# Gate columns of the modulation as running sums on VectorE instead of column-tiled products on TensorE

## Chip, cores and metric

One core of one Trainium2 chip runs the kernel. The metric is the device time of one execution in microseconds; three runs of the kernel before gave 3354.97, 3355.01 and 3358.41 us, with a median of 3355.01 us.

## What is computed

One layer of a diffusion block over 384 token columns: 128 context tokens (prompt) and 256 latent tokens (sample). Everything is float32. Cut to what matters:

```python
mod = silu(c_ctx) @ w_ada + b_ada        # prompt;  sample: silu(c) @ w_ada + b_ada
shift, scale, gate = split(mod, 3)       # each 4096 wide; w_ada is 4096 x 12288
u = rms_norm(h, norm_w) * (1 + scale) + shift
proj = u @ w_in                          # 4096 x 16448: inputs of 8 retention and 16 delta-rule heads, and 64 gate columns
mixed, states = mixers(proj)             # two bidirectional recurrences in chunks, with a triangular solve
h = h + gate * (mixed @ w_out)           # w_out is 4096 x 4096
y = rms_norm(h, final_norm_w)
```

The change is about `gate`: 4096 columns of `mod`, for two conditioning vectors (prompt and sample). They are needed only in the last line, when the output projection's columns are finished, 512 at a time.

## The kernel before

**Weights.** Every large product is split in two parts for precision. A piece is one block of 128 rows of weights by 512 columns. SyncE (SP) loads two pieces at a time into a tile `raw` (ring of three, L197), ScalarE rounds it to `wh` (L209), VectorE forms the remainder `wl = raw - wh` (L210), and TensorE runs nine matmuls of 512 columns (kind N, L264 to L266) or twelve of 384 (kind T, L258 to L260) on a piece. `wh` and `wl` have rings of five (`RING`), and `run_pieces` (L347) writes the loads and splits of a piece into the program up to four pieces ahead of its matmuls. All engines work their instructions strictly in program order; SP runs as far ahead as ring slots come free.

**Stages.** First (to about 770 us) the shift and scale columns of `mod` and the first parts of the input projection run together; class `Ada` (L301) makes the products with `w_ada`, from a ring `adar` of six tiles of 512 KB. Then `open_mixers` starts the mixer stage: the 32 groups of columns of `w_in` are finished in eight periods p = 0 to 7 of four groups each, two of kind T and two of kind N. Since some parts were done in the first stage, the periods hold 56, 128, 96, 84, 108, 100, 96 and 112 pieces. Last comes the output projection: eight blocks of 512 columns with 32 pieces each, `w_out`.

**Background work.** The mixers of period p (generators `gdn` and `ret`) are put into the program between the matmuls. `slot(ns)` advances a planned TensorE time; whenever the planned time of a background step has passed, `bg_step` writes the next one. Each `yield ns` gives a step's expected VectorE time; `pace` multiplies it by 1.4 and by a factor from 0.5 to 1 that depends on when the result is due. A piece counts 1920 ns, and an `Ada` piece 450 ns. Background work and `wl` share VectorE, in program order. The longest VectorE part is the triangular solve, `gdn` L851 to L857: 30 steps of one TENSOR_TENSOR (L854) and one TENSOR_REDUCE (L856) each, after a wait for the tile `M` that comes back from DRAM through the GpSimd (POOL) queue. Below, "a solve" is the stretch from its first to its last VectorE instruction; there is one in each period.

**Gate columns before.** `Ada` also makes the gate columns, in the N groups of the mixer stage: eight blocks of 512 columns, 16 pieces each, 128 pieces in all. A piece loads 512 rows by 256 columns (512 KB) into a slot of the ring `raw`, and runs

```python
for q in range(4):
    k = i % NK + q
    PE.matmul(self.ps[32 * q:32 * q + 32, cs], cst[:, 2 * k:2 * k + 32], raw[:, q, 0], ...,
              tile_position=(0, 32 * q))
```

on four column tiles of the array (L322; eight matmuls in the trace, since a float32 product takes two). These pieces take one of the four places for prepared pieces, and their `raw` slot comes free only when TensorE has run them. At the end of a block, `gate_done` copies the four partial sums out (L1178), adds them up with a 0/1 matrix `sel` (L1184), fetches the bias with two DMAs on the POOL queue (L1188), adds it on VectorE (L1191) and writes `d_gate` to DRAM (L1192). These steps are "urgent": they go ahead of other background steps.

**Output.** For every block of 512 output columns, `pre` (in `out_done`) loads `d_gate` five pieces before the block's end.

Of the kernel before, what the change touches and what calls it, by code (L numbers as in the profile page):

```python
# [7 lines left out]
F32 = mybir.dt.float32  # L8
F32R = mybir.dt.float32r
AF = mybir.ActivationFunctionType  # L10
ALU = mybir.AluOpType
# [4 lines left out]
D = 4096  # L16
NK = 32
T = 384
# [23 lines left out]
ADA_RING = 6  # L42
RAW_LIVE = 8
SLOT = 1000.0
PRE = 5
RING = 5
PACE = 1.4
# [5 lines left out]
GATE = 1500  # L53
# [6 lines left out]
LEAD = 3  # L60
WAIT1 = 5000
# [4 lines left out]
def hybrid_step(ctx: ExitStack, tc: tile.TileContext, x_prompt, x_sample, state_ret_fwd, state_ret_bwd,  # L66
# [35 lines left out]
    half_c = const.tile([128, 2, 12], F32, name="half_c")  # L102
    mid_ctx = ExitStack()
# [5 lines left out]
    cst = mid.tile([128, 2 * NK + 32], F32, name="cst")  # L109
    sel = mid.tile([128, 2], F32, name="sel")  # L110
# [10 lines left out]

    G.memset(half_c[:, 0], -0.5)
# [68 lines left out]

    def load_piece(src, chunks, k0, nk, ring=None):
        shape = [128, nk, len(chunks), chunks[0][1]]
        if ring:
            raw = ring(shape)
        else:
            raw = wpool.tile(shape, F32, tag="raw", name="raw", bufs=3)  # L197
        for i, (c0, cn) in enumerate(chunks):
            SP.dma_start(out=raw[:, :, i, :],
                         in_=src[k0 * 128:(k0 + nk) * 128, c0:c0 + cn].rearrange("(k p) n -> p k n", p=128))  # L200
        return raw

    def split_tile(raw, shape, place=None):
# [5 lines left out]
        A.copy(h, raw)  # L209
        V.tensor_tensor(lo, raw, h.bitcast(F32), op=ALU.subtract)  # L210
        return h, lo
# [89 lines left out]
    class Ada:  # L301
# [6 lines left out]
        def __init__(self, c0, width, ps_alloc, done, ring=None):  # L308
# [7 lines left out]
        def compute(self, i, raw):  # L316
            if self.ps is None:
                self.ps = self.ps_alloc()
            cs = slice(256 * (i // NK), 256 * (i // NK) + 256)
            for q in range(4):  # L320
                k = i % NK + q
                PE.matmul(self.ps[32 * q:32 * q + 32, cs], cst[:, 2 * k:2 * k + 32], raw[:, q, 0],  # L322
                          start=(k < 4), stop=(k >= NK - 4), tile_position=(0, 32 * q))
# [23 lines left out]
    def run_pieces(pieces):  # L347
# [9 lines left out]
        kind = lambda o: "do" if isinstance(o, Do) else ("ada" if isinstance(o, Ada) and o.ring else "w")  # L357
# [14 lines left out]
    crow = st.tile([64, 128], F32, name="crow")  # L372
# [5 lines left out]
    V.tensor_copy(sel, con[:, C_SEL:C_SEL + 2])  # L378
# [9 lines left out]
    brow = st.tile([64, 128], F32, name="brow")  # L388
    nrow = st.tile([32, 128], F32, name="nrow")
    grow = st.tile([1, 128], F32, name="grow")  # L390
# [280 lines left out]
    def gates(graw):  # L671
# [4 lines left out]
        par = mx.tile([128, 5, 16], F32, tag="mix", name="par", bufs=2)  # L676
# [63 lines left out]
    def u3(ap):  # L740
        return ap.rearrange("p (n t) -> p n t", n=3)

    def gdn(p, rt):
# [257 lines left out]
        for i, h in enumerate(heads):  # L1001
            so = mx.tile([128, 2, 128], F32, tag="mix", name="so", bufs=2)
# [45 lines left out]
        for i, h in enumerate(heads):  # L1048
# [4 lines left out]
            t = mx.tile([128, T], F32, tag="mix", name="mix", bufs=2)  # L1053
            V.scalar_tensor_tensor(out=t, in0=ps[:, 0:T], scalar=gnw[:, 0:1], in1=zT[:, i], op0=ALU.mult, op1=ALU.mult)
            G.dma_start(out=d_mix[16 + h], in_=t)
            yield

    def ret(h, rt):
# [104 lines left out]
        for a in range(2):  # L1163
# [4 lines left out]
            t = mx.tile([128, T], F32, tag="mix", name="mix", bufs=2)  # L1168
# [4 lines left out]

    def gate_done(i):
        def done(ps):
            sb = [mx.tile([128, T], F32, tag="gsb", name="gsb", bufs=2)[:, 0:256] for _ in range(2)]
            for j in range(2):
                A.copy(sb[j], ps[:, 256 * j:256 * j + 256])  # L1178
            urgent.append(fin(ps, sb))

        def fin(ps, sb):
            yield GATE
            for j in range(2):
                PE.matmul(ps[0:2, 256 * j:256 * j + 256], sel, sb[j], start=True, stop=True)  # L1184
            yield
            c0 = 512 * i
            for j in range(2):
                G.dma_start(out=sb[j][0:2], in_=b_ada[0, 2 * D + c0 + 256 * j:2 * D + c0 + 256 * j + 256].partition_broadcast(2))  # L1188
            yield 2000
            for j in range(2):  # L1190
                V.tensor_tensor(sb[j][0:2], ps[0:2, 256 * j:256 * j + 256], sb[j][0:2], op=ALU.add)  # L1191
                G.dma_start(out=d_gate[:, c0 + 256 * j:c0 + 256 * j + 256], in_=sb[j][0:2])  # L1192
        return done
# [20 lines left out]
    ada_q = []  # L1214
    for i in range(8):
        ada_q += Ada(2 * D + 512 * i, 512, lambda: ps_main.tile([128, 512], F32, tag="mm3", name="adg"), gate_done(i)).pieces
    for g, (kind, chunks) in enumerate(groups):
        k0 = reached.get(g, 0)
        pre, done = sum_done(g, ("dram" if g >= 4 else "sbuf") if k0 else None, True)
        gm = Gemm(kind, w_in, chunks, list(range(k0, NK)), done, pre)  # L1220
        if g % 4 == 0 and g:
            dues[id(gm), max(0, len(gm.pieces) - PRE)] = ("gdn", g // 4 - 1)
        if kind == "T":
            pieces += gm.pieces
        else:
            n, rest = len(gm.pieces), 0
            if g % 2:
                rest = min(8, n // 2)
                cnt = len(ada_q) - 16 * (7 - g // 4)
            else:  # L1230
                cnt = min(16, max(0, 16 * n // (n + NK - reached.get(g + 1, 0) - 8)))
            pieces += gm.pieces[:LEAD] + interleave(gm.pieces[LEAD:n - rest], ada_q[:cnt]) + gm.pieces[n - rest:]
            ada_q = ada_q[cnt:]
    assert not ada_q
# [16 lines left out]

    oc = {}
# [28 lines left out]
    def out_done(c0):  # L1281
# [3 lines left out]
        def pre():  # L1285
# [3 lines left out]
            op = oc["sb"]  # L1289
            box["x"] = op.tile([128, 3, 512], F32, tag="xo", name="xo", bufs=1)  # L1290
# [29 lines left out]

    for i in range(8):
# [7 lines left out]
        if i == 0:  # L1329
# [4 lines left out]
            for j, piece in enumerate(seq):  # L1334
# [3 lines left out]
                pieces.append(piece)  # L1338
        else:
            pieces += gm.pieces  # L1340
# [53 lines left out]
```

## Time and profile before

| what | value |
|---|---|
| median of three runs | 3355.01 us |
| profiled execution: its own time | 3351.84 us |
| profiled execution: span from first to last instruction | 3350.1 us |
| mean granted TensorE clock | 0.991 |
| mean DMA rate over the span | 187 GB/s |

The profile names an instruction group by line, engine, operation and tiles (`out<-in`). PE is the matmul row of TensorE and PEld its weight loads, DVE is VectorE, ACT ScalarE, POOL GpSimd, SP SyncE. Busy times are the union of instruction times in microseconds, means are in nanoseconds. A waits row reads "who waits <- for whom: us in total, times, longest".

### The profile page before, as it was taken

Reading aid. Unit: us, or ns where it says so; the run is one execution under the profiler, and the core shown is the slowest. Engines: PE = TensorE matmul, PEld = TensorE weight load, DVE = VectorE, ACT = ScalarE, POOL = GpSimd, SP = SyncE. Lnnn points to the kernel's source line nnn. Section 1 sums busy time; section 2 is a strip of 40 time slices with the busy share of each in tenths; the row PEclk is TensorE's granted clock in tenths of the full one; section 3 lists DMA queues with packets and bytes.
Section 4 is the critical chain, followed back from the end, with each engine's and each line's share of the span. In section 5 each row is a group of like instructions: output and inputs, shape, how many; then the busy total and the mean of one; then the engine's idle time right before and its main releaser. Section 6 shows DMA issues by size and latency. Waiting matters only on the chain.

```text
span 3350.1 us, 51853 instructions
## 1 busy us (share of the span) xinstructions
PE 3254.2 (97%) x19312; PEld 2694.5 (80%) x19312; DVE 1845.3 (55%) x3811; ACT 1201.5 (36%) x2588; POOL 292.7 (9%) x463
## 2 busy tenths in 40 slices
PE   5999999999999999999999999999999999999998
PEld 2878888877799789689689689779779877788886
DVE  3664444337747646755756746746744855444444
ACT  3322222224244344244244244245244334333333
POOL 0000000001011011001011011011000002100000
PEclk7999999999999999999999999999999999999999
DMA  9989998965535545545644545554544555645445
GB/s 327 308 289 303 324 303 282 303 189 171 160 92 151 166 138 167 167 142 150 186 145 143 172 138 152 173 156 141 172 152 142 159 153 186 188 145 169 146 150 176
DMA packets 594237, 626.14 MB, mean 187 GB/s; under 512 B 38978, under 2 KB 577042, under 8 KB 593984
## 3 DMA queue, kind: packets, MB, share of 16 engines
q1 hardware_dynamic: 570096, 551.04, 52.0%
q0 software_dynamic: 23888, 71.79, 7.2%
q8 instruction: 151, 2.47, 0.3%
q14 instruction: 102, 0.84, 0.1%
HBM read 590.37 MB, written 32.33 MB: 186 GB/s over the span
## 4 chain that ended last, share of the span: by engine, by line
PE 81%; DVE 7%; DMA 6%; issue 3%; ACT 1%; SPq 1%; POOL 0%; ACTq 0%; POOLq 0%; DVEq 0%
PE mm L258 11%; PE mm L260 10%; PE mm L259 10%; PE mm L264 10%; PE mm L265 9%; PE mm L266 9%; PE ada L322 3%; DMA raw<-in_w_in_dram 3%; DVE tmp L854 3%; PE o L265 2%; PE o L266 2%; PE o L264 2%; DVE wl L210 2%; DMA mixl<-d_mix 2%; PE adg L322 1%
## 5 line engine op out<-in xcount | busy, mean ns | idle before, releaser
L210 DVE TENSOR_TENSOR wl<-raw,wh 128x512 fp32r<-128x512 f32 x1274 | 855.3, 686 | 947.4 <-ACT wh L209 931.6
L209 ACT CAST wh<-raw 128x512 fp32r<-128x512 f32 x1274 | 757.5, 620 | 1388.5 <-DMA raw<-in_w_in_dram 567.7
L264 PE MATMUL mm<-wh,uh 128*128 128x512 f32 x1920 | 782.4, 408 | 12.3 <-ACT rawt L564 5.9
L265 PE MATMUL mm<-wl,uh 128*128 128x512 f32 x1920 | 756.5, 394 | 18.0 <-DVE wl L210 17.4
L266 PE MATMUL mm<-wh,ul 128*128 128x512 f32 x1920 | 751.6, 391 | 0.0
L258 PE MATMUL mm<-uh,wh 128*128 128x384 f32 x2048 | 716.8, 350 | 4.1 <-DVE ul L555 2.7
L260 PE MATMUL mm<-uh,wl 128*128 128x384 f32 x2048 | 685.8, 335 | 0.0
L259 PE MATMUL mm<-ul,wh 128*128 128x384 f32 x2048 | 685.1, 335 | 0.0
L264 PEld LDWEIGHTS mm<-wh,uh 128*128 128x128 f32 x1920 | 361.3, 188 | 144.9 <-issue 44.2
L265 PEld LDWEIGHTS mm<-wl,uh 128*128 128x128 f32 x1920 | 361.7, 188 | 103.5 <-DVE wl L210 36.4
L258 PEld LDWEIGHTS mm<-uh,wh 128*128 128x128 f32 x2048 | 384.7, 188 | 48.7 <-issue 25.0
L266 PEld LDWEIGHTS mm<-wh,ul 128*128 128x128 f32 x1920 | 361.1, 188 | 76.7 <-DVE ul L1249 0.3
L259 PEld LDWEIGHTS mm<-ul,wh 128*128 128x128 f32 x2048 | 385.1, 188 | 3.9 <-issue 2.9
L260 PEld LDWEIGHTS mm<-uh,wl 128*128 128x128 f32 x2048 | 384.4, 188 | 0.0
L854 DVE TENSOR_TENSOR tmp<-M 48x4 f32<-48x4 f32 (+14 forms) x240 | 188.3, 784 | 3.4
L322 PE MATMUL ada<-adar,cst 128*32 128x256 f32 x2048 | 146.8, 403 | 23.4 <-DMA adar<-in_w_ada_dram 23.4
L645 DVE SCALAR_TENSOR_TENSOR acc<-rawt,cw,acc 128x126 f32<-128x126 f32 (+3 forms) x384 | 133.5, 410 | 11.9 <-ACT acc L640 11.9
L265 PE MATMUL o<-wl,uh 128*128 128x512 f32 x354 | 138.1, 390 | 0.9 <-DVE wl L210 0.9
L264 PE MATMUL o<-wh,uh 128*128 128x512 f32 x354 | 137.9, 389 | 1.0 <-ACT wh L209 1.0
L266 PE MATMUL o<-wh,ul 128*128 128x512 f32 x354 | 137.7, 389 | 0.0
L856 DVE TENSOR_REDUCE M<-tmp 48x2 f32<-48x4 f32 (+14 forms) x240 | 121.7, 507 | 8.4
L322 PEld LDWEIGHTS ada<-adar,cst 128*32 128x32 f32 x2048 | 53.8, 112 | 88.7 <-DMA adar<-in_w_ada_dram 42.9
(321 smaller groups left out, 2522.5 us busy)
## 6 DMA issues: line engine op xcount, KB each, us to landing
raw<-in_w_in_dram SPq DMA_DIRECT2D x1028, 256.0 KB, 3.7
adar<-in_w_ada_dram SPq DMA_DIRECT2D x256, 512.0 KB, 5.4
raw<-in_w_ada_dram SPq DMA_DIRECT2D x128, 512.0 KB, 3.7
raw<-in_w_out_dram SPq DMA_DIRECT2D x256, 256.0 KB, 3.1
rawt<-d_part POOLq DMA_DIRECT2D x26, 384.0 KB, 4.3
d_part<-spill POOLq DMA_DIRECT2D x9, 768.0 KB, 6.3
gr<-d_gc POOLq DMA_DIRECT2D x16, 384.0 KB, 7.3
d_mix<-mix POOLq DMA_DIRECT2D x32, 192.0 KB, 2.8
```

Of the source, the lines that this page charges most:

```text
L209: A.copy(h, raw)
L210: V.tensor_tensor(lo, raw, h.bitcast(F32), op=ALU.subtract)
L258: PE.matmul(ps, wh, high(k), start=st, stop=False)
L259: PE.matmul(ps, wh, low(k), start=False, stop=False)
L260: PE.matmul(ps, wl, high(k), start=False, stop=sp)
L264: PE.matmul(ps, a, h, start=st, stop=False)
L265: PE.matmul(ps, a, lo, start=False, stop=False)
L266: PE.matmul(ps, b, h, start=False, stop=sp)
L322: PE.matmul(self.ps[32 * q:32 * q + 32, cs], cst[:, 2 * k:2 * k + 32], raw[:, q, 0], start=(k < 4), stop=(k >= NK - 4), tile_position=(0, ...
L645: V.scalar_tensor_tensor(out=dst[:, lo:hi], in0=x[:, lo + o:hi + o], scalar=w(t), in1=dst[:, lo:hi], op0=ALU.mult, op1=ALU.add)
L854: V.tensor_tensor(t, M[0:48, 0:i, 0:i].rearrange("p j c -> p c j"), M[0:48, i:i + 1, 0:i].to_broadcast([48, i, i]), op=ALU.mult)
L856: V.tensor_reduce(M[0:48, i, 0:i], t, axis=AX.X, op=ALU.add)
```

## The change

The class `GateSum` takes the place of `Ada` for the gate columns. A piece loads two blocks of 128 rows by 384 columns (384 KB, into `raw`). VectorE multiplies each block by the per-partition conditioning value and adds it to a running sum of 128 x 384, one for each of the two vectors: four instructions a piece, two of them (`add(0)`) written at once and two (`add(1)`) behind the next `wl`. There are eleven blocks (ten of 384 columns and one of 256) of 16 pieces, so 176 pieces and 704 instructions. When a block is full, four matmuls with a matrix of ones (each on a column tile of 32) sum over the partitions, four DMAs bring the bias, one VectorE addition and four more DMAs finish it.

One block runs in each of periods 1 to 7, spread evenly over all four groups of the period but its first 3 and last 10 pieces; the other four run in the output projection, spread over its blocks 1 to 6. `GateSum` pieces count 0 ns of planned TensorE time and no place among the prepared pieces.

To make room, the ring `raw` goes from three to four, the ring `adar` of the first stage from six to five, and several tiles of the mixers are written over others that have been read: `vn` over `vT`, `so` over `kt`, the mixed output over `zT` and over `rt["q"]`; `con2`, `par` and small start-up tiles change places. The diff, cut:

```diff
-ADA_RING = 6
+ADA_RING = 5
+RAW_RING = 4
+GATE_W = 384
+GATE_END = 10
...
-            raw = wpool.tile(shape, F32, tag="raw", name="raw", bufs=3)
+            raw = wpool.tile(shape, F32, tag="raw", name="raw", bufs=RAW_RING)
...
         A.copy(h, raw)
         V.tensor_tensor(lo, raw, h.bitcast(F32), op=ALU.subtract)
+        if later:
+            later.pop(0)()
         return h, lo
...
+    class GateSum:
+        slots = 0.0
+        def __init__(self, c0, width):
+            self.c0, self.width = c0, width
+            self.pieces = [(self, i) for i in range(0, NK, 2)]
+        def prepare(self, i):
+            raw = load_piece(w_ada, [(2 * D + self.c0, self.width)], i, 2)
+            if i == 0:
+                tag = (lambda v: f"ga{v}") if oc else (lambda v: "gsb")
+                self.acc = [(oc["sb"] if oc else mx).tile([128, T], F32, tag=tag(v), name="gacc", bufs=2)
+                            for v in range(2)]
+            def add(q):
+                for v, acc in enumerate(self.acc):
+                    a, w = acc[:, 0:self.width], cst[:, 2 * (i + q) + v:2 * (i + q) + v + 1]
+                    if i + q == 0:
+                        V.tensor_scalar(a, raw[:, q, 0], scalar1=w, scalar2=None, op0=ALU.mult)
+                    else:
+                        V.scalar_tensor_tensor(out=a, in0=raw[:, q, 0], scalar=w, in1=a, op0=ALU.mult, op1=ALU.add)
+            while later:
+                later.pop(0)()
+            add(0)
+            if i + 2 < NK:
+                later.append(lambda: add(1))
+            else:
+                add(1)
+        def compute(self, i, hl):
+            if i + 2 == NK:
+                urgent.append(self.fin())
+            return 1
+        def fin(self):
+            n, sb = self.width // 2, self.acc[0]
+            parts = [(32 * q, q // 2, n * (q % 2)) for q in range(4)]
+            yield GATE
+            ps = ps_main.tile([128, T // 2], F32, tag="mm3", name="gsum")
+            for r, v, o in parts:
+                PE.matmul(ps[r:r + 32, 0:n], ones, self.acc[v][:, o:o + n], start=True, stop=True, tile_position=(0, r))
+            yield
+            for r, v, o in parts:
+                c0 = 2 * D + self.c0 + o
+                G.dma_start(out=sb[r:r + 32, 0:n], in_=b_ada[0, c0:c0 + n].partition_broadcast(32))
+            yield 2000
+            V.tensor_tensor(sb[:, 0:n], ps[:, 0:n], sb[:, 0:n], op=ALU.add)
+            for r, v, o in parts:
+                G.dma_start(out=d_gate[v:v + 1, self.c0 + o:self.c0 + o + n], in_=sb[r:r + 1, 0:n])
+            clock["gate"] = self.c0 + self.width
...
-        kind = lambda o: "do" if isinstance(o, Do) else ("ada" if isinstance(o, Ada) and o.ring else "w")
+        kind = lambda o: "do" if isinstance(o, (Do, GateSum)) else ("ada" if isinstance(o, Ada) else "w")
...
-            t = mx.tile([128, 3, 128], F32, tag="vn", name="vn", bufs=2)
+            t = u3(vT[:, i])
...
-            so = mx.tile([128, 2, 128], F32, tag="mix", name="so", bufs=2)
+            so = kt[i][:, 0:2]
...
-            V.scalar_tensor_tensor(out=t, in0=ps[:, 0:T], scalar=gnw[:, 0:1], in1=zT[:, i], op0=ALU.mult, op1=ALU.mult)
-            G.dma_start(out=d_mix[16 + h], in_=t)
+            V.scalar_tensor_tensor(out=zT[:, i], in0=ps[:, 0:T], scalar=gnw[:, 0:1], in1=zT[:, i], op0=ALU.mult, op1=ALU.mult)
+            G.dma_start(out=d_mix[16 + h], in_=zT[:, i])
...
-            t = mx.tile([128, T], F32, tag="mix", name="mix", bufs=2)
+            t = rt["q"][:, T * a:T * a + T]
...
+    gate_sums = [GateSum(c0, min(GATE_W, D - c0)).pieces for c0 in range(0, D, GATE_W)]
+    for p in range(8):
+        gp = []
+        for g in range(4 * p, 4 * p + 4):
...
+            gp += gm.pieces
+        if p:
+            gp = gp[:LEAD] + interleave(gp[LEAD:-GATE_END], gate_sums.pop(0)) + gp[-GATE_END:]
+        pieces += gp
...
+        elif i < 7:
+            behind += gm.pieces
         else:
-            pieces += gm.pieces
+            pieces += interleave(behind, [p for ps in gate_sums for p in ps]) + gm.pieces
```

More of the change, by code (lines that the diff above doesn't have):

```diff
@@ L102, in hybrid_step @@
     half_c = const.tile([128, 2, 12], F32, name="half_c")
+    ones = const.tile([128, 32], F32, name="ones")
+    cst = const.tile([128, 2 * NK + 32], F32, name="cst")
     mid_ctx = ExitStack()
@@ L108, in hybrid_step @@
     gnw = mid.tile([128, 1], F32, name="gnw")
-    cst = mid.tile([128, 2 * NK + 32], F32, name="cst")
-    sel = mid.tile([128, 2], F32, name="sel")
     rcon = mid.tile([128, R_N], F32, name="rcon")
@@ L120, in hybrid_step @@
     rk_dec = mid.tile([128, 2, 8], F32, name="rk_dec")
+    G.memset(ones, 1.0)
     G.memset(half_c[:, 0], -0.5)
@@ L189, in slot @@
             clock["next"] = max(clock["next"], -SLOT) + bg_step()
+    oc = {}
     def load_piece(src, chunks, k0, nk, ring=None):
@@ L201, in load_piece @@
         return raw
+    later = []
     def split_tile(raw, shape, place=None):
@@ L306, in hybrid_step, with __init__ @@
         slots = 450.0
-        def __init__(self, c0, width, ps_alloc, done, ring=None):
+        def __init__(self, c0, width, ps_alloc, done, ring):
             self.c0, self.width, self.ps_alloc, self.done, self.ring = c0, width, ps_alloc, done, ring
@@ L371, in hybrid_step @@
     con = st.tile([128, C_N], F32, tag="spill", name="con", bufs=2)
-    crow = st.tile([64, 128], F32, name="crow")
+    boot = st.tile([64, 4, 128], F32, tag="spill", name="boot", bufs=2)
+    crow = boot[:, 0]
     SP.dma_start(out=con, in_=consts)
@@ L377, in hybrid_step @@
     V.tensor_copy(neg.rearrange("p d s -> p (d s)"), con[:, C_NF:C_NF + 256])
-    V.tensor_copy(sel, con[:, C_SEL:C_SEL + 2])
     def psb():
@@ L386, in hybrid_step @@
     A.activation(cst[:, 0:2 * NK].rearrange("p (k b) -> p b k", b=2), ps[:, 0:64].rearrange("p (b k) -> p b k", b=2), AF.Silu)
-    brow = st.tile([64, 128], F32, name="brow")
-    nrow = st.tile([32, 128], F32, name="nrow")
-    grow = st.tile([1, 128], F32, name="grow")
+    brow, nrow, grow = boot[:, 1], boot[0:32, 2], boot[0:1, 3]
     vrow = st.tile([120, 2, 128], F32, tag="u32", name="vrow", bufs=2)
@@ L675, in gates @@
         con = mx.tile([128, 3, 128], F32, tag="acc", name="con2", bufs=2)
-        par = mx.tile([128, 5, 16], F32, tag="mix", name="par", bufs=2)
+        par = mx.tile([128, 5, 16], F32, tag="d15", name="par", bufs=2)
         G.dma_start(out=con[:, 0:2], in_=consts[:, C_TF:C_TF + 256].rearrange("p (a b) -> p a b", a=2))
@@ L1167, in ret @@
             yield
-            t = mx.tile([128, T], F32, tag="mix", name="mix", bufs=2)
+            t = rt["q"][:, T * a:T * a + T]
             (A.copy if a else V.tensor_copy)(t, ps[:, 0:T])
@@ L1171, in ret @@
         yield
[L1174 to L1193, printed above, removed]
     def gates_done(ps):
@@ L1213, in hybrid_step @@
     pieces += Do(open_mixers).pieces + Gates(gates_done).pieces
[L1214 to L1223, printed above, removed]
-            pieces += gm.pieces
[L1225 to L1234, printed above, removed]
+    gate_sums = [GateSum(c0, min(GATE_W, D - c0)).pieces for c0 in range(0, D, GATE_W)]
+    for p in range(8):
+        gp = []
+        for g in range(4 * p, 4 * p + 4):
+            kind, chunks = groups[g]
+            k0 = reached.get(g, 0)
+            pre, done = sum_done(g, ("dram" if g >= 4 else "sbuf") if k0 else None, True)
+            gm = Gemm(kind, w_in, chunks, list(range(k0, NK)), done, pre)
+            if g % 4 == 0 and g:
+                dues[id(gm), max(0, len(gm.pieces) - PRE)] = ("gdn", g // 4 - 1)
+            gp += gm.pieces
+        if p:
+            gp = gp[:LEAD] + interleave(gp[LEAD:-GATE_END], gate_sums.pop(0)) + gp[-GATE_END:]
+        pieces += gp
     rowk = [(2 * (j // 4) if j % 4 >= 2 else 16 + 2 * (j // 4)) + j % 2 for j in range(NK)]
@@ L1249, in mix_put @@
         V.tensor_tensor(low(j), mixl[j], high(j).bitcast(F32), op=ALU.subtract)
-    oc = {}
     def open_out():
@@ L1289, in pre @@
             op = oc["sb"]
+            assert clock["gate"] >= c0 + 512
             box["x"] = op.tile([128, 3, 512], F32, tag="xo", name="xo", bufs=1)
@@ L1319, in place @@
                            for t in (uh, ul)]
+    behind = []
     for i in range(8):
```

1 line of the change is left out of this document (removed).

## Prediction

> **What bounds the kernel now.** I read the page's totals first, then one gate piece in the timeline, then the groups of instructions, a table of windows by solve and by stage, and last the waits.
>
> ```profile
> span 3350.1 us, 51853 instructions
> ...
> PE 3254.2 (97%) x19312; PEld 2694.5 (80%) x19312; DVE 1845.3 (55%) x3811; ACT 1201.5 (36%) x2588; POOL 292.7 (9%) x463
> ```
>
> TensorE's matmul row is busy nearly throughout, VectorE a little over half. So work taken off TensorE should shorten the run, as long as VectorE, in program order, still delivers `wl` in time. What a gate piece costs TensorE is read in the timeline (start, length in us, instruction).
>
> ```profile
> 776.92 0.39 PE L265 MATMUL mm<-wl,uh 128*128 128x512 f32 x1
> 777.15 0.39 PE L266 MATMUL mm<-wh,ul 128*128 128x512 f32 x1
> 777.47 0.64 PE L322 MATMUL adg<-raw,cst 128*32 128x256 f32 x8
> 778.04 0.50 PE L264 MATMUL mm<-wh,uh 128*128 128x512 f32 x1
> 778.37 0.39 PE L265 MATMUL mm<-wl,uh 128*128 128x512 f32 x1
> 778.61 0.39 PE L266 MATMUL mm<-wh,ul 128*128 128x512 f32 x1
> ```
>
> A plain step takes 0.23 (776.92 to 777.15). From the L266 before the piece to the L266 behind it, three steps on, 1.46 pass instead of 0.68. The eight matmuls and the stop and restart around them thus cost 0.78 us.
>
> ```profile
> L322 PE MATMUL adg<-raw,cst 128*32 128x256 f32 x1024 | 81.8, 391 | 2.1 <-DMA raw<-in_w_ada_dram 2.1
> ```
>
> 1024 matmuls are 128 pieces: 128 x 0.78 = 100 us of TensorE time that the change removes. That is the most that the trace prices directly.
>
> ```profile
> core 0: us, PE busy (x) PEld busy (x) DVE busy (x) ACT busy (x) POOL busy (x), PEclk, DMA share, GB/s
> ...
> sum 447.80, PE 424.59 PEld 305.33 DVE 405.04 ACT 99.87 POOL 2.04; mean PE 53.07 PEld 38.17 DVE 50.63 ACT 12.48 POOL 0.25
> ```
>
> This table has one window per solve (from its first to its last instruction on VectorE), eight in all; the sum says that VectorE is busy 405.0 of 447.8, which is 50.6 of 56.0 us in each. Here VectorE, not TensorE, is nearly full. The next three answers split those windows: the solves' own tile `M`, the gate matmuls, and `wl` in the first and the last window.
>
> ```profile
> sum 447.80, DVE 310.44 POOL 0.00; mean DVE 38.80 POOL 0.00
> ```
>
> ```profile
> sum 447.80, PE 38.40 PEld 9.41 DVE 0.82 ACT 0.64; mean PE 4.80 PEld 1.18 DVE 0.10 ACT 0.08
> ```
>
> ```profile
> 843.40:897.10 53.70, 24.73 (x61) 11.26 (x61) 14.02 (x22) 1.00 0.54 167
> ...
> 2630.80:2685.80 55.00, 27.85 (x72) 13.34 (x71) 14.13 (x22) 1.00 0.54 168
> ```
>
> Of the 50.6 us the solve takes 310.4 / 8 = 38.8, and 22 `wl` take the other 11.8, or 0.54 each. The gate matmuls' 38.4 us at 0.64 a piece are 60 pieces, 7.5 a window. TensorE's need in a window is then 22 pieces of nine steps (2.05 each, 45 us) and 7.5 x 0.78 = 5.9, together 51 of 56: it loses about 5 us in each solve already.
>
> **The change, part by part.** *Removed from TensorE:* 100 us, of which 60 x 0.78 = 47 lie in the solves and 53 outside.
>
> *Added to VectorE:* 704 instructions of 128 x 384. The trace has this operation with 126 to 255 columns on SBUF tiles and with 384 from PSUM:
>
> ```profile
> L210 DVE TENSOR_TENSOR wl<-raw,wh 128x512 fp32r<-128x512 f32 x1274 | 855.3, 686 | 947.4 <-ACT wh L209 931.6 <-PE ada L322 7.5 <-PE mm L259 2.8
> ...
> L645 DVE SCALAR_TENSOR_TENSOR acc<-rawt,cw,acc 128x255 f32<-128x255 f32 x96 | 45.8, 477 | 0.0
> ...
> L645 DVE SCALAR_TENSOR_TENSOR acc<-rawt,cw,acc 128x126 f32<-128x126 f32 x96 | 33.0, 344 | 11.9 <-ACT acc L640 11.9
> ...
> L1054 DVE SCALAR_TENSOR_TENSOR mix<-bg,gnw,rawt 128x384 f32<-128x384 f32 x16 | 9.7, 612 | 3.8 <-PE bg L1051 3.6
> ```
>
> The slope (477 - 344) / (255 - 126) = 1.03 ns a column gives 610 for 384, and L1054 shows 612. But instructions in a row overlap at their ends:
>
> ```profile
> 1010.95 2.05 DVE L645 SCALAR_TENSOR_TENSOR acc<-rawt,cw,acc 128x126 f32<-128x126 f32 x6
> 1012.92 0.69 DVE L210 TENSOR_TENSOR wl<-raw,wh 128x512 fp32r<-128x512 f32 x1
> ```
>
> Three of 0.344 and three of 0.477 are 2.46 by their lengths and 2.05 as a row, 0.07 less each. I take 0.54, so 2.16 a gate piece and 704 x 0.54 = 380 us in all, with 0.61 as the upper end. [...] The row above shows starts closer together than the lengths, so I keep to the row.
>
> Where does this go? By stage:
>
> ```profile
> 770.00:2785.00 2015.00, 1981.57 (x11682) 1656.18 (x11681) 1245.29 (x2694) 783.97 (x1791) 228.87 (x343) 1.00 0.51 154
> 2860.00:3300.00 440.00, 436.00 (x1918) 359.30 (x1917) 189.18 (x284) 146.55 (x263) 25.14 (x44) 1.00 0.52 160
> ```
>
> In the mixers VectorE is busy 1245 of 2015 us; seven blocks add 7 x 64 x 0.54 = 242 (1487). In the output projection it is 189 of 440, and four blocks add 138 (327, or 74%). On average both fit. Outside the solves the mixers go from 840 of 1567 (1245 - 405, 2015 - 448) to about 1017 of 1510. TensorE has `wl` four pieces ahead, 8 us, against crowded places such as the convolutions; I allow 10 us for new stalls there (0 to 30) and 5 in the output projection (0 to 20).
>
> *The solves are where it doesn't fit.* Periods 1 to 7 have 724 pieces, less 13 each at the ends 633, and 112 gate pieces over them: 0.18 for each piece. Background steps are placed by planned TensorE time; as 7.5 `Ada` pieces of 450 ns leave a window, 1.8 more ordinary ones enter, 23.8 in all. VectorE then needs 38.8 + 23.8 x 0.54 + 4.2 x 2.16 = 60.7 us, TensorE 23.8 x 2.05 = 48.8. VectorE is 11.9 too slow, and only the lead softens it. Part of that is gone at the start, because the solve first waits for `M`:
>
> ```profile
> ACT wh L209 <- DMA raw<-in_w_in_dram: 421.6, 125, 8.5
> ...
> PEld mm L265 <- DVE wl L210: 36.4, 54, 3.3
> ...
> DVE M L851 <- DMA M<-d_m: 31.6, 8, 6.9
> ```
>
> 31.6 / 8 = 4.0 us a solve, so 4.2 of the 8.2 us lead remain and TensorE stalls 7.7, against 5 now. In each of seven windows 5.9 is saved and 2.7 lost: 7 x 3.2 = 22. The solve of period 0 gets no gate piece; I count 8 for it, since both its gate pieces and part of its stall go.
>
> *The ring.* The first row says that ScalarE (and `wl` behind it) waits for raw weights 421.6 / 125 = 3.4 us at a time. One reason stands in SP's own waits:
>
> ```profile
> SPq L199 <- PE adg L322: 197.4, 76, 6.6
> ```
>
> Gate pieces now hold a `raw` slot until TensorE has run them, and SP can't load. After the change VectorE frees the slot, and there are four. I count 5 us for that (0 to 40, which is the 5 us of all eight solves).
>
> *The first stage* loses one of six `adar` tiles. It costs TensorE little waiting now (from 100 us to the stage's end):
>
> ```profile
>   DMA adar<-in_w_ada_dram: 7.4, 26
> ```
>
> ```profile
> adar<-in_w_ada_dram SPq DMA_DIRECT2D x256, 512.0 KB, 5.4
> raw<-in_w_ada_dram SPq DMA_DIRECT2D x128, 512.0 KB, 3.7
> ```
>
> Five tiles in flight are still nearly as many as land in 5.4 us at the stage's rate; I count 2 us lost (-5 to 10).
>
> *Finishing a block.* Four small matmuls and their stop on TensorE replace four others of the same kind:
>
> ```profile
> 882.24 1.02 PE L1184 MATMUL adg<-gsb,sel 128*2 128x256 f32 x4
> 883.20 0.50 PE L264 MATMUL mm<-wh,uh 128*128 128x512 f32 x1
> ```
>
> Eleven blocks instead of eight at some 1 us each cost 3 at most; as each product is narrower I count 0. Four bias DMAs follow each other on the POOL queue instead of two:
>
> ```profile
>   DMA gsb<-in_b_ada_dram: 5.2, 8
> ...
> L1188 POOL DMA_DIRECT2D gsb<-in_b_ada_dram x16: 499/530/574, 883.1 to 2777.8; - x16
> ...
> DMA to landing us min/median/max: 1.6/3.5/5.2
> ```
>
> 4 x 0.53 + 3.5 is 5.6 us, while the addition is written 2 us behind, so VectorE may stand still 3.6 us, with the next `wl` behind it; the lead of 8.2 covers it. I count 2 us for the eleven (40 if a block ends with no lead).
>
> *In-place tiles.* They cost no instruction. A later `rawt` now waits for the `d_mix` transfer out of it; POOL loads parts five pieces (10 us) before they are added, so a wait of the length below is covered; uncovered it would cost that much for a group, some 20 us over the periods.
>
> ```profile
> d_mix<-mix POOLq DMA_DIRECT2D x32, 192.0 KB, 2.8
> ```
>
> The loads of gate columns, 176 of 384 KB for 128 of 512, run on SP beside a half-idle DMA.
>
> Sum: 22 + 8 + 53 + 5 gained, 10 + 5 + 2 + 2 lost: 69 us. The profiled execution took 3351.8 us (1.7 outside the span), 3.2 under the median; 3355 - 69 = 3286.
>
> **Rivals.** *A: VectorE loses the lead altogether (about no change).* With 0.61 an instruction, `wl` at its full 0.69 and no lead left, a solve is 38.8 + 16.4 + 10.2 = 65.4 against 48.8: 16.6 lost, less 5 now, 81 in seven. With 20 more in the crowded places outside, 100 - 81 - 20 leaves nothing: 3355. For it speaks that the solves are 90% full now, against it that VectorE has slack on average, so the lead comes back between crowded places. [...] The timeline, with step after step at 0.23, speaks against it; I leave it 0.03 of A's chance.
>
> *B: the additions wait for their own data (slower).* `add(0)` is written right behind its load, so VectorE, in order, would wait for 384 KB to land, with all `wl` and background steps behind it. Weights make ScalarE wait 3.4 us at a time now. If each gate piece cost VectorE 3.4, a solve would lose 4.2 x 3.4 = 14 more, 100 in seven, and in the output projection 64 x 3.4 + 327 = 545 us would exceed the 440: 105 more. 3286 + 205 = 3491. It turns into a loss where the wait passes 2.3 us a piece in the solves (69 / 29.4). Against it: with four slots of two pieces, SP can start a load some 6 to 12 us before it is read, and it lands in 3.7 (above); in the output projection such waits are few today:
>
> ```profile
> ACT wh L209 <- DMA raw<-in_w_out_dram: 32.4, 14, 4.1
> ```
>
> *C: better.* If the fourth slot and the end of TensorE-held slots remove the 5 us stalls of the solves and the lead takes in the rest, the 100 us stay whole and some 10 come on top: 3245.
>
> **How the numbers follow.** My forecast 0.66, C 0.14, A 0.11, B 0.09. The range is 3238 to 3340: up to 54 us above the forecast (20 more in the crowded places, 15 more in the output projection, 8 in the first stage, some 11 where a block's end or a transfer is not covered), and 48 below (40 of the ring and 7 of the first stage), which takes C in. A and B, 0.20, stay outside. A measurement here can tell 0.2%, 7 us, from no change. Faster by more: 0.66 + 0.14 + 0.05 of A = 0.85; the same 0.05; slower 0.10 (B and the end of A).
>
> **What would show it.** The matmuls of L322 named `adg` are gone, 704 additions of about 0.6 us stand on VectorE, and VectorE's share is near 68%. In the solves VectorE is busy over 95% and TensorE waits for `wl` more than the 36.4 us of now. The waits of additions for `w_ada` transfers are short. In the output projection TensorE stays full. Wrong would be: additions that idle over 1 us each before they start (B), solves far longer than 62 us or long `wl` waits outside them (A), a first stage that ends later by over 10 us.

## The result, and the profile after

Slower. Four runs of the changed kernel have a median of 3388.94 us (3385.96 to 3392.01), four of the kernel before 3354.99 us. The ratio is 1.0099, with a 95% interval of 1.0081 to 1.0116: about 33 us lost where 69 gained were forecast, and 49 us beyond the end of the range. The profiled execution took 3386.23 us.

The page's totals after the change, and three of its rows of groups (a row ends with the engine's idle time ahead of the group and what ended it):

```profile
span 3384.5 us, 50821 instructions
...
PE 3199.1 (95%) x18344; PEld 2694.1 (80%) x18344; DVE 2179.9 (64%) x4509; ACT 1198.8 (35%) x2572; POOL 320.5 (9%) x520
...
L218 DVE TENSOR_TENSOR wl<-raw,wh 128x512 fp32r<-128x512 f32 x1274 | 854.5, 686 | 717.7 <-ACT wh L217 697.3
...
L275 PE MATMUL mm<-wl,uh 128*128 128x512 f32 x1920 | 766.4, 399 | 71.3 <-DVE wl L218 70.9
...
L362 DVE SCALAR_TENSOR_TENSOR gacc<-raw,cst,gacc 128x384 f32<-128x384 f32 (+1 forms) x682 | 379.9, 600 | 8.7 <-DMA raw<-in_w_ada_dram 8.7
```

The 968 matmuls are gone (19312 to 18344) and with them 55 us of TensorE's busy time, yet the span is 34 us longer: TensorE now stands still more. The 682 additions (the other 22 of 704 start a sum with a plain product) cost VectorE what was forecast, 380 us (379.9 in the trace), and waited only 8.7 us for their own data. So VectorE's own bill was right; what it does to TensorE was not. Of the signs that the prediction listed, these came as written: L322's matmuls gone, solves over 95% busy on VectorE and near 62 us long, short waits of additions for `w_ada`. VectorE's share is 64% where 68% was listed. Two that would be wrong came as well: a first stage that ends over 10 us later, and an output projection that is no longer full.

The answer on waits for the whole kernel (waiter, what it waited for, us in total, times, longest):

```profile
PEld mm L275 <- DVE wl L218: 114.5, 107, 3.0
...
DVE M L913 <- DMA M<-d_m: 33.9, 8, 6.2
...
DVE gacc L388 <- DMA gacc<-in_b_ada_dram: 12.7, 10, 2.0
```

TensorE's weight loads wait 114.5 us for `wl`, against 36.4 before; some 110 of the 114.5 lie in the eight solves and the 4 us behind each. The four bias DMAs of a block's end make VectorE wait 12.7 us in all.

Where the time went is read by cutting both executions at the same weight matmuls. The windows by stage (first stage, period 0, periods 1 to 7, blocks 1 to 6 of the output projection; start:end length, then busy time of each engine, granted clock, DMA share, GB/s), first of the kernel before, then of the kernel after:

```profile
0.00:769.00 769.00, 725.54 (x5223) 588.70 (x5224) 348.04 (x719) 217.18 (x434) 18.55 (x41) 0.97 0.87 288
769.00:898.50 129.50, 121.40 (x604) 85.75 (x602) 98.91 (x230) 48.47 (x115) 13.40 (x19) 1.00 0.57 173
898.50:2800.70 1902.20, 1875.06 (x11152) 1582.68 (x11153) 1155.66 (x2485) 742.00 (x1690) 218.09 (x328) 1.00 0.51 153
2876.70:3271.50 394.80, 392.91 (x1730) 324.12 (x1729) 166.10 (x248) 128.44 (x229) 17.62 (x31) 1.00 0.51 157
```

```profile
0.00:790.50 790.50, 733.82 (x5224) 594.27 (x5225) 342.33 (x719) 213.68 (x435) 18.57 (x42) 0.99 0.89 281
790.50:906.70 116.20, 105.92 (x470) 84.04 (x468) 97.42 (x228) 47.67 (x111) 11.87 (x15) 1.00 0.42 120
906.70:2810.00 1903.30, 1812.37 (x10260) 1571.10 (x10260) 1374.66 (x2921) 745.51 (x1671) 231.61 (x356) 0.99 0.49 146
2889.90:3304.50 414.60, 403.54 (x1762) 327.98 (x1761) 284.55 (x502) 124.28 (x229) 30.57 (x58) 0.98 0.68 207
```

Period 0 is 13.3 us shorter. Periods 1 to 7 take the same time with some 890 fewer matmuls, so nothing that TensorE saved there arrived. The first stage is 21.5 longer and blocks 1 to 6 are 19.8 longer; block 0 adds 3.9, block 7 nothing.

Periods 1 to 7, cut once more, at the weight matmuls between which the solve of the changed kernel stands: from the first that starts behind the solve's start to the first that starts 4 us behind its end. All traces have the same weight matmuls in the same order, so the same ones cut every kernel (sums over seven periods, from their start times):

| us | in front of the solve | solve stretch | behind it |
|---|---|---|---|
| kernel before | 862.1 | 432.4 | 607.7 |
| kernel after | 883.6 | 456.1 | 563.5 |

Behind the solve 44 us were gained, in the solves 24 lost, in front 21 lost.

### The profile page after: what moved, and what is told of

It reads as the page before. It is cut to its first block, busy times and chain, and to the rows that moved or that the text cites. A ratio compares the mean times of both kernels' runs of the same rounds, so it can differ in the third digit from the quotient of the medians.

```text
span 3384.5 us, 50821 instructions
## 1 busy us (share of the span) xinstructions
PE 3199.1 (95%) x18344; PEld 2694.1 (80%) x18344; DVE 2179.9 (64%) x4509; ACT 1198.8 (35%) x2572; POOL 320.5 (9%) x520
## 5 line engine op out<-in xcount | busy, mean ns | idle before, releaser
L275 PE MATMUL mm<-wl,uh 128*128 128x512 f32 x1920 | 766.4, 399 | 71.3 <-DVE wl L218 70.9
L275 PEld LDWEIGHTS mm<-wl,uh 128*128 128x128 f32 x1920 | 364.4, 190 | 182.9 <-DVE wl L218 114.5
L274 PEld LDWEIGHTS mm<-wh,uh 128*128 128x128 f32 x1920 | 363.9, 190 | 111.4 <-ACT rawt L626 13.7
L276 PEld LDWEIGHTS mm<-wh,ul 128*128 128x128 f32 x1920 | 363.7, 189 | 74.8 <-DVE ul L1282 0.3
L362 DVE SCALAR_TENSOR_TENSOR gacc<-raw,cst,gacc 128x384 f32<-128x384 f32 (+1 forms) x682 | 379.9, 600 | 8.7 <-DMA raw<-in_w_ada_dram 8.7
```

The lines of the kernel that those rows point to most:

```text
L274: PE.matmul(ps, a, h, start=st, stop=False)
L275: PE.matmul(ps, a, lo, start=False, stop=False)
L276: PE.matmul(ps, b, h, start=False, stop=sp)
L362: V.scalar_tensor_tensor(out=a, in0=raw[:, q, 0], scalar=w, in1=a, op0=ALU.mult, op1=ALU.add)
```

## The experiments

My theory after the result: in the solves VectorE is the bound, so every microsecond of additions placed there is a microsecond of TensorE; the five-tile ring costs the first stage its 20 us; gate loads and additions hold up the output projection. The rivals: the loads, not the additions, cost the mixers their time (slots and traffic), or the start-up and ring edits cost it all.

The eight kernels down to the rings ran once each, beside one run of the kernel before on the same chip (in brackets). They are read by their stages more than by their whole times.

**The kernel before, once more.** This second profile shows how far stage lengths vary by themselves.

> The kernel before once more, profiled on the chip of the next three, to see how far the first stage moves by itself from chip to chip. If the 21.5 us of the changed kernel's first stage are the change's, this one ends the stage within 4 us of 769; if it ends at 775 or later, a part of them was the chip.

3358.46 us (3353.52 for the other run on that chip). First stage 771.2, period 0 131.4, periods 1 to 7 863.7 / 432.1 / 608.9, blocks 1 to 6 392.9. So a stage repeats within 2 to 3 us in these two profiles, and I read differences of 5 us and more.

**Without the additions.** Only the first product of each sum is made; the loads and the ends of blocks stay, the gate columns are not summed.

```diff
                         V.tensor_scalar(a, raw[:, q, 0], scalar1=w, scalar2=None, op0=ALU.mult)
-                    else:
-                        V.scalar_tensor_tensor(out=a, in0=raw[:, q, 0], scalar=w, in1=a, op0=ALU.mult, op1=ALU.add)
```

> The changed kernel with the gate columns' additions left out (only the first multiplication of each block is kept; all loads and block ends stay), so 682 of 704 VectorE instructions are gone. Theory V (VectorE's time for the additions makes the new stalls in the mixers and the output projection): solves return to 52 us or less, the mixers from 790 us on lose about 60 to 90 us, the output projection 10 to 20, the whole is near 3300. Theory L (the loads of gate columns, their slots and traffic make the stalls): it stays within 15 us of 3386.

3290.32 us (before: 3358.91). Period 0 116.1, periods 1 to 7 864.3 / 381.3 / 560.4. What was removed from TensorE is worth 13.3 + 51.1 + 47.3 - 2.2 = 109.5 us in the mixers; 100 to 105 were forecast. The additions then take 74.8 back in the solves, 19.3 in front of them and 3.1 behind. The windows of the eight solves show why. First the changed kernel (one row of eight, and the sum), then the one without additions:

```profile
1611.90:1673.30 61.40, 52.14 (x212) 39.96 (x211) 59.97 (x101) 14.61 (x24) 0.00 (x0) 0.97 0.45 134
...
sum 477.60, PE 406.42 PEld 303.92 DVE 465.44 ACT 111.15 POOL 0.00; mean PE 50.80 PEld 37.99 DVE 58.18 ACT 13.89 POOL 0.00
```

```profile
1578.40:1629.40 51.00, 48.36 (x208) 38.29 (x206) 49.58 (x81) 14.93 (x24) 0.00 (x0) 1.00 0.46 136
...
sum 420.30, PE 398.71 PEld 317.22 DVE 406.74 ACT 118.31 POOL 0.00; mean PE 49.84 PEld 39.65 DVE 50.84 ACT 14.79 POOL 0.00
```

VectorE is 97% busy in both (465.4 of 477.6, 406.7 of 420.3). At 0.23 a matmul TensorE needs 212 x 0.23 = 49 us in the first row and 48 in the second: it loses some 13 of 61 and 3 of 51. The 20 additions of that solve, in the same windows restricted to the tile `gacc`, are about the difference:

```profile
1611.90:1673.30 61.40, 0.00 (x0) 0.00 (x0) 11.26 (x20) 0.00 (x0) 0.97 0.45 134
```

One expectation failed: the output projection should have become 10 to 20 us shorter, and blocks 1 to 6 got 5 us longer (419.7).

**Half of the additions.** Only the sums of the first vector are made.

```diff
-                    else:
+                    elif v == 0:
                         V.scalar_tensor_tensor(out=a, in0=raw[:, q, 0], scalar=w, in1=a, op0=ALU.mult, op1=ALU.add)
```

> The changed kernel with the additions of the second conditioning vector left out (but for the first of each block): half of VectorE's new work, all loads and block ends. If the solves have no lead left to give, their cost is in proportion: 456 - 381 = 75 us for all additions, so 35 to 40 for half (solve stretches at 416 to 421), and the stretches in front 10. If a lead softens it, as the prediction had it (4.2 us a solve), half the additions cost far less than half: solve stretches under 400. Whole: about 3335 in the first case, 3315 in the second.

3324.41 us (before: 3353.52). Periods 1 to 7: 866.9 / 424.1 / 564.7. Half of the additions cost the solves 42.8 us of the 74.8 (57%). A lead that took in part of the load would have made the first half nearly free; instead the cost is close to proportional from the first addition on. In the stretches of this kernel the additions keep VectorE busy for 39.1 us, in those of the changed kernel for 74.2. In front of the solves it is otherwise: the first half costs 2.6, the second 16.7. There a cover exists and runs out.

**Without the loads.** Only the first piece of a block is loaded; the additions read their own sum, so the gate values are left out.

```diff
-            raw = load_piece(w_ada, [(2 * D + self.c0, self.width)], i, 2)
             if i == 0:
+                raw = load_piece(w_ada, [(2 * D + self.c0, self.width)], i, 2)
...
-                        V.scalar_tensor_tensor(out=a, in0=raw[:, q, 0], scalar=w, in1=a, op0=ALU.mult, op1=ALU.add)
+                        V.scalar_tensor_tensor(out=a, in0=a, scalar=w, in1=a, op0=ALU.mult, op1=ALU.add)
```

> The changed kernel with the loads of gate columns left out but for the first of each block; the additions read their own sum instead, so VectorE's work is the same and 63 MB are not fetched. Theory V: solves stay at 61 us, the mixers within 10 us, the whole at 3370 to 3386. Theory L: waits of ScalarE for raw weights fall well under the 564 us and the whole falls to 3320 or less. If the output projection's 20 us come from traffic and not from VectorE, that stage alone gets them back here and not in the run without additions.

3372.82 us (before: 3358.91). Periods 1 to 7: 883.7 / 455.5 / 562.2, within 1.3 us of the changed kernel in each part. In the mixers the loads cost nothing, and that rival falls there. Blocks 1 to 6 drop from 414.6 to 404.1: there the loads cost about 10.

**Gate pieces kept out of the solves.** They go into the two groups ahead of the one with the solve and the one behind it.

```diff
-            gp = gp[:LEAD] + interleave(gp[LEAD:-GATE_END], gate_sums.pop(0)) + gp[-GATE_END:]
+            a, b, n = cut[2], cut[3], len(gp) - GATE_END
+            gs = gate_sums.pop(0)
+            k = 16 * (a - LEAD) // max(1, a - LEAD + max(0, n - b))
+            if n > b:
+                gp = gp[:LEAD] + interleave(gp[LEAD:a], gs[:k]) + gp[a:b] + interleave(gp[b:n], gs[k:]) + gp[n:]
+            else:
+                gp = gp[:LEAD] + interleave(gp[LEAD:a], gs[:15]) + gp[a:n] + gs[15:] + gp[n:]
```

> The changed kernel with the gate pieces of periods 1 to 7 kept out of the third group of each period, where the solve stands; the same 16 pieces go over the two T groups and the last group. Theory V in its sharp form (an addition inside a solve costs TensorE its whole VectorE time, elsewhere little): the stretches of the solves, together 456 us in the changed kernel and 381 without additions, return to 400 or less; the stretches in front of them, 884, get at most 25 longer, since 7 x 4.3 pieces move there. Whole: 3325 to 3345. Rival (VectorE is short everywhere, so the cost only moves): stretches in front grow by 60 or more and the whole stays at 3375 to 3390.

3349.71 us (before: 3353.52). Periods 1 to 7: 895.8 / 395.5 / 575.4. The solves give back 60.6 us, and the same additions cost 12.2 in front and 11.9 behind. Moving them along the program thus gains 36 us with no instruction less. The whole misses the 3345 that I gave as its upper end by 5 us.

What the additions cost in each part of periods 1 to 7, against the kernel without them, beside the time for which they keep VectorE busy in that part (its instructions on `gacc`):

| us: cost / busy | in front of the solve | solve stretch | behind it |
|---|---|---|---|
| half of the additions | 2.6 / 76.8 | 42.8 / 39.1 | 4.3 / 23.9 |
| changed kernel | 19.3 / 136.7 | 74.8 / 74.2 | 3.1 / 43.7 |
| pieces kept out of the solves | 31.5 / 163.6 | 14.2 / 13.7 | 15.0 / 77.1 |

In the solve stretches the additions cost about their whole time, whether they are many or few; elsewhere they cost about a fifth of it or less. So the place decides most of the price, but the work isn't free anywhere: 61 of the 97 us stay.

**The rings of the first stage, and the start-up tiles.** Two kernels are the one before with one edit each; the third is the changed kernel with both rings as before.

```diff
-ADA_RING = 6
+ADA_RING = 5
```

> The kernel before with one edit: five tiles of 512 KB in the ring of the first stage instead of six. In the changed kernel the first stage ends 21.5 us later than before (first matmul of the mixers' N group at 790.5 instead of 769.0). If the smaller ring is the cause, this kernel is about 20 us slower than before (3370 to 3380) and the mixers and the output projection keep their lengths. If the cause is another edit of the first stage (start-up tiles that share a slot, the raw ring of four), it stays within 5 us of 3355.

```diff
-    crow = st.tile([64, 128], F32, name="crow")
+    boot = st.tile([64, 4, 128], F32, tag="spill", name="boot", bufs=2)
+    crow = boot[:, 0]
...
-    brow = st.tile([64, 128], F32, name="brow")
-    nrow = st.tile([32, 128], F32, name="nrow")
-    grow = st.tile([1, 128], F32, name="grow")
+    brow, nrow, grow = boot[:, 1], boot[0:32, 2], boot[0:1, 3]
```

> The kernel before with the small start-up tiles put into one tile in a slot of the ring `spill`, as in the changed kernel, and nothing else. If this edit delays the first stage, the first matmul of the input projection starts some 2 us later and the stage ends 5 us or more later than in the run of the kernel before; otherwise both agree within 3 us.

```diff
-ADA_RING = 5
+ADA_RING = 6
...
-RAW_RING = 4
+RAW_RING = 3
```

> The changed kernel with the ring sizes of before (six in the first stage, three for raw). If the ring of the first stage is the cause there, it ends near 769 us again (-20). The mixers and the output projection then show what the fourth raw slot is worth with gate sums: if it matters, they get 10 to 40 us longer; if not, the whole is near 3365.

The first stage ends at 779.7 with the ring of five alone (kernel before: 769.0 and 771.2), at 770.1 with the start-up tiles alone, and at 776.3 with both rings back, where the whole took 3454.86 us (before: 3358.91). The other two took 3363.26 (3358.91) and 3359.78 (3353.52). So the ring costs 9 to 11 us of the first stage, half of what I expected, and the start-up tiles nothing there. The rival that these edits cost it all is left with the first stage at most. SyncE's queue in the first stage and the waits of ScalarE and of TensorE's weight loads (100 to 770 us) show what the shorter ring changes, and what not. Kernel before:

```profile
SPq L199 <- PE ada L322: 312.7, 115, 8.3
```

```profile
ACT wh L209 <- DMA raw<-in_w_in_dram: 131.6, 45, 7.8
...
PEld mm L258 <- ACT wh L209: 14.2, 28, 3.1
...
PEld ada L322 <- DMA adar<-in_w_ada_dram: 7.0, 25, 0.9
```

The kernel before with a ring of five:

```profile
SPq L199 <- PE ada L322: 377.7, 118, 7.3
```

```profile
ACT wh L209 <- DMA raw<-in_w_in_dram: 314.7, 77, 11.8
...
PEld ada L322 <- DMA adar<-in_w_ada_dram: 6.1, 11, 1.4
PEld mm L258 <- ACT wh L209: 6.1, 8, 3.2
```

SyncE issues both streams in turn (in the kernel before `adar` loads at 306.8 us, `raw` at 307.8, `adar` again at 312.6, `raw` at 314.8). With five tiles it stands 65 us longer waiting for a free `adar` tile, and the `w_in` loads queued behind come late: ScalarE waits 314.7 us for them instead of 131.6. But that lateness doesn't show as a longer wait of TensorE for `wh`: its weight loads wait 6.1 us for it instead of 14.2. The loss falls early. Against the first profile of the kernel before, 8.4 of 10.7 us are lost by the 1000th weight matmul (310 us there), and from the first weight matmul (60 us) to there TensorE's matmul row waits 5.0 us for `adar` tiles instead of 1.4, its weight loads 8.9 instead of 3.6. So about 4 of the 8 are waits for the ring's own tiles; where the others come from stays open.

Raw slots matter at the other end: with three, blocks 1 to 6 take 471.2 us instead of 414.6, and the parts in front of the solves 906.0 instead of 883.6. The fourth slot is needed by this change.

**Both repairs together.** Gate pieces out of the solves, ring of six with four raw slots; the constants `rcon` move to the mixers' memory to make room.

```diff
-ADA_RING = 5
+ADA_RING = 6
...
-    rcon = mid.tile([128, R_N], F32, name="rcon")
...
-        G.dma_start(out=rcon, in_=rconsts)
...
+        rcon = mx.tile([128, R_N], F32, name="rcon")
+        G.dma_start(out=rcon, in_=rconsts)
```

> The gate pieces kept out of the solves' groups, as in the run before, and the ring of the first stage back at six beside a raw ring of four (3.6 KB for it come from a constant tile that is now loaded when the mixers open). If the ring of five is what delays the first stage, it ends 10 us or more earlier than the 793 of the run with a ring of five, and the whole is 3335 to 3340, 0.4 to 0.6% faster than the kernel before. If the delay comes from the fourth raw slot, the first stage stays at 790 and the whole near 3350.

3335.26 us, ratio 0.9941 (0.9924 to 0.9958): faster than both kernels, some 20 us under the kernel before. The first stage ends at 775.6, periods 1 to 7 take 898.7 / 400.1 / 573.4, blocks 1 to 6 413.2.

**The output projection.** First its gate pieces closer together, in the middle of each block, away from the block's end and its operand loads (0.48 a piece).

```diff
-            pieces += interleave(behind, [p for ps in gate_sums for p in ps]) + gm.pieces
+            gs = [p for ps in gate_sums for p in ps]
+            for j in range(6):
+                b, n = behind[32 * j:32 * j + 32], 11 if j < 4 else 10
+                pieces += b[:3] + interleave(b[3:25], gs[:n]) + b[25:]
+                gs = gs[n:]
+            pieces += gm.pieces
```

> As the run above, and in the output projection the gate pieces are kept out of the first 3 and last 7 pieces of each block, where the loads of output operands on the POOL queue run. If those loads and the gate loads together delay the weights there, blocks 1 to 6 fall from 413 us to 400 or less and the whole by another 10 us. If the additions are then too dense for VectorE between (0.48 a piece), the blocks get longer, 420 or more.

3351.36 us, ratio 0.9984 (0.9974 to 0.9995): 16 us worse than the kernel that it was made from, and blocks 1 to 6 go from 413.2 to 429.6. Closer together is worse.

Then a ring of their own, so that gate loads take no slot from `w_out`.

```diff
-            raw = load_piece(w_ada, [(2 * D + self.c0, self.width)], i, 2)
+            own = oc and (lambda shape: oc["sb"].tile([128, 1, 1, GATE_W], F32, tag="gw", name="gw", bufs=3)[:, :, :, 0:self.width])
+            if own:
+                half = [load_piece(w_ada, [(2 * D + self.c0, self.width)], i + q, 1, own)[:, 0, 0] for q in range(2)]
...
-            t = oc["sb"].tile([128, 512], F32, tag="to", name="to", bufs=3)
+            t = oc["sb"].tile([128, 512], F32, tag="to", name="to", bufs=2)
```

> This is e9 (ring of six, raw ring of four, gate pieces kept out of the solves) with one more edit, in the output projection alone: the gate columns are loaded one block of 128 rows at a time (192 KB) into a ring of three small tiles of their own, and the raw ring of four serves only w_out there; to make room two output tiles stand instead of three. Theory 1, the gate loads hold up the w_out loads because they share the raw slots: blocks 1 to 6 of the output projection fall from 413 to 403 us or less, ScalarE's waits for w_out there fall under 60 us, the whole goes from 3335 to about 3325. Theory 2, traffic and VectorE's own time are the cost, whoever owns the slots: blocks 1 to 6 stay at 410 or more, the whole within 5 us of e9.

3334.91 us, ratio 0.9937 (0.9921 to 0.9954); blocks 1 to 6 take 412.8 us, 0.4 less. ScalarE's waits for `w_out` (2880 to 3300 us) fall a little and the stage does not follow. Here they are for the changed kernel, for the kernel that this one was made from, for this one, and for the one without loads:

```profile
ACT wh L217 <- DMA raw<-in_w_out_dram: 114.7, 42, 9.5
```

```profile
ACT wh L216 <- DMA raw<-in_w_out_dram: 112.0, 39, 9.6
```

```profile
ACT wh L216 <- DMA raw<-in_w_out_dram: 90.1, 33, 8.7
```

```profile
ACT wh L217 <- DMA raw<-in_w_out_dram: 5.0, 2, 3.0
```

Shared slots are not the cause, and the third output tile isn't missed: ScalarE and VectorE wait 62.7 us at `to` here and 62.3 in the kernel that it was made from. Without loads the waits are gone, and 9 of the 20 us stay (404.1); with half of the additions the stage takes 404.0; with loads and no additions it is longer, 419.7. The loads have a part; the additions have one only without the loads, and the parts don't add up.

## Why the prediction was wrong, point by point

- *128 x 0.78 = 100 us off TensorE*: right. The kernel without additions gained 109.5 us in the mixers. The 0.03 of A's chance was given to TensorE being limited by its weight loads; no run shows that. They are 80% busy in the kernel before and 82% in the one without additions, whose time fell by 69 us.
- *704 x 0.54 = 380 us on VectorE*: right (379.9 and 8.2 for the 22 products). *Rival B* falls with it: additions waited for their own data 8.7 us in all.
- **The solves** (forecast: 22 us gained; measured: 24 lost). The need was right: 60.7 us forecast, 61.1 measured as the mean of periods 1 to 7 ((477.6 - 49.7) / 7), VectorE full. The step that failed is "only the lead softens it", with "4.2 of the 8.2 us lead remain and TensorE stalls 7.7". TensorE loses some 13, and the additions cost their whole VectorE time: 74.8 us for 74.2 us of additions in the solve stretches, 42.8 for 39.1 with half of them, 14.2 for 13.7 with most of them moved away. No lead shows in any of the three. The prediction held the counter-evidence itself. It read that TensorE loses 5 us in each solve already; an engine with 4.2 us of lead left would not stall while VectorE needs 50.6 of 56. That stall said that the lead was spent, so added work was to be charged in full. This is rival A's mechanism, which had 0.11, inside the solves alone: A also had long `wl` waits outside them, and those are some 4 of the 114.5 us. *C*, in which the stalls of the solves go, is excluded by the same rows.
- **Crowded places outside** (forecast: 10, 0 to 30): 19.3 in front of the solves and 3.1 behind, mis-sized within its bounds.
- **The first stage** (forecast: 2, -5 to 10; measured: 21.5). The step that failed is "five tiles in flight are still nearly as many as land", sized by TensorE's waits for `adar` tiles from 100 us on, 7.4 us. In the kernel with the ring of five alone that row is 8.6, nearly the same; the loss falls mostly before 310 us and in part before 100, and about half of it isn't a wait for these tiles. The ring of five alone costs 9 to 11. With four raw slots beside it the stage ends at 786 to 793 (five kernels), with six and four at 774 to 776 (three kernels), so with four raw slots the five tiles cost 11 to 19. The last 5 us against the kernel before stay open; the start-up tiles and the fourth slot are ruled out.
- **The output projection** (forecast: 5, 0 to 20; measured: 19.8 in blocks 1 to 6). The average of VectorE (285 of 415 us busy) said that it fits. What I can account for is, against the kernel before, 9.2 us more in which the matmul row stands still (414.6 - 403.5 against 394.8 - 392.9 in the windows by stage), up to 6.8 us of half clock (below), and 2.7 for four block ends: at 3100 us, 0.67 pass there beyond the ordinary steps. Together that is 18.7 of the 19.8, if none of it overlaps. TensorE's weight loads wait 9.0 us for `wl` and 7.6 for `wh` there, 2.1 and 1.4 before, so the waits are of both kinds, VectorE and ScalarE with its data, and which of the new loads and additions makes them is open.
- *Finishing a block* (2 us) and *in-place tiles* (0): nothing speaks against them. 12.7 us of bias waits lie on VectorE. The kernel without additions has the in-place edits too, and its mixers gained the whole 100. The in-place edits weren't tried alone.
- *The ring of four* (5 us gained): the removal came out some 5 to 10 over the 100, as that would have it, but it was not taken apart. The range's lower end takes these 5 us twice: 40 is the whole of that term, and 35 of it were left below the forecast.

In sum, 69 us gained became 33 lost: 46 of the difference in the solves, 20 in the first stage, 19 in the output projection with its first block, and the rest, 18, outside the solves in the mixers. The two placements that the runs could mend (solves, ring) make a kernel of 3335 us. That is the most that a kernel here got out of the idea: some 110 off TensorE, and 90 still paid for elsewhere.

## What to carry to other kernels

Where an engine already stalls its consumer in some stretch, the lead in front of that stretch is spent: charge all work added there at full price (here 74.8 us for 74.2 us of additions), whatever the engine's average is, and place fillers by stretch, not evenly. Where a ring gets shorter, look for the part of the stage in which its reader waits, its start above all (here 8.4 of 10.7 us were lost by 310 us); and a wait that grows much on another engine (ScalarE's 183 us here) need not be what costs. A kernel that leaves out only the added work separates the removal from the addition in one run.

## What the runs showed of the hardware

A short stall of TensorE can cost more than its length. The timeline of TensorE in the changed kernel, near the end of a solve (start, length, instruction, idle time before it):

```profile
1658.72 0.40 PE L274 MATMUL mm<-wh,uh 128*128 128x512 f32 x1
1660.92 0.50 PE L275 MATMUL mm<-wl,uh 128*128 128x512 f32 x1 [1.81 <-DVE wl L218]
1661.26 0.50 PE L276 MATMUL mm<-wh,ul 128*128 128x512 f32 x1
1661.56 0.63 PE L274 MATMUL mm<-wh,uh 128*128 128x512 f32 x1
1661.99 0.63 PE L275 MATMUL mm<-wl,uh 128*128 128x512 f32 x1
```

After 1.81 us of idle time the steps go from 0.23 to 0.43: the granted clock has halved (0.5 for 3.41 us in the trace's clock record). The same in the output projection, after a late `wl`:

```profile
2898.66 0.80 PE L275 MATMUL o<-wl,uh 128*128 128x512 f32 x1 [4.34 <-DVE wl L218]
2899.25 0.63 PE L276 MATMUL o<-wh,ul 128*128 128x512 f32 x1
2899.68 0.63 PE L274 MATMUL o<-wh,uh 128*128 128x512 f32 x1
...
2903.91 0.39 PE L275 MATMUL o<-wl,uh 128*128 128x512 f32 x1
2904.14 0.39 PE L276 MATMUL o<-wh,ul 128*128 128x512 f32 x1
```

Between 100 us and the end of the matmuls, the trace's clock record has 13 such spells of 3.4 or 6.8 us at half clock in the changed kernel, 51.2 us together, against two with 6.8 us in the kernel before (five with 20.5 in its second profile). At half speed that is at most 26 us of TensorE against 3 to 10: as a consequence of the stalls, at most some 15 to 22 of the 33 us come through the clock, and less where VectorE holds TensorE up anyway. The mean clock, 0.990 against 0.991, doesn't show it, since the profile of the kernel before has 41 us at half clock in its first 60 us. In the example above 1.81 us of idle time was enough, and each of the 15 spells of the changed kernel and of the first profile of the kernel before has idle time of 1.8 to 3.3 us in the 3.4 us ahead of it. Such idle time doesn't always do it: of the 16 stalls of 1.8 us or more in the changed kernel, 13 are followed by a spell, and of five in the kernel before, two.

While VectorE waited for the solve's `M` it took nothing that stands later in the program. In the kernel before the `wh` of a piece was ready at 2099.82 us; VectorE then stood still for 6.92 us, until `M` came at 2106.85, and made the `wl` of that piece only at 2107.23, behind the solve's first step.
